# Decay rows by plain broadcasts, half-size differences and other small moves of order in a hybrid decoder layer

## The chip, the cores and the metric

The kernel runs on one core of a Trainium2 chip. The metric is the device time of one execution in microseconds (us); each kernel is run several times, and the median counts. Engines are named as in the profile: PE (TensorE, matmuls; PEld is its weight load), DVE (VectorE), ACT (ScalarE), POOL (GpSimd), SP (SyncE, whose in-order queue issues nearly all transfers).

## The reference

One decoder layer over 1024 tokens of width 1024, in float32. Two groups of heads read one input projection and mix tokens in parallel; their outputs are joined by one output projection, and a squared-ReLU MLP of hidden width 4096 follows.

```python
h = rms_norm(x, norm1_w)
proj = h @ w_in                      # q,k,v of 4 attention heads; q,k,v,z,a,b of 4 DeltaNet heads
# group A: differential attention, causal, two 64-d softmax maps per head, 128-d values
da_o = (softmax(q1 k1^T) - lam * softmax(q2 k2^T)) v     # then per-head rms_norm
# group B: gated DeltaNet: causal conv (width 4) + SiLU on q,k,v, L2-normed q,k, decay g, strength beta
#   chunked delta rule; within a chunk decay[i,j] = exp(G_i - G_j) for j <= i, else 0 (G: running sum of g)
x = x + concat(da_o, dn_o) @ w_out
x = x + square(relu(rms_norm(x, norm2_w) @ w_up)) @ w_down
```

## The kernel before, in words

Every large product is made in three matmuls of float32 parts: each operand is split into a rounded part (`hH`, `wH`, by a cast on ACT) and the rest (`hL`, `wL`, by a subtraction on DVE or POOL), and PE adds high x high, high x low and low x high. So each weight tile is loaded by SP (`wraw`, `raw`, `dw`), cast by ACT, subtracted, then used.

The stages in order of time, with where they lie in the profiled execution:

- *Norm and gate projection* (0 to 60 us). Blocks of 128 tokens: `z_norm(tb)` squares on ACT, takes the power on POOL and scales on DVE (L249) to `hn`; `to_hT` transposes it on PE; `z_part(tb, u)` multiplies by two weight units `wz[0]`, `wz[1]`, rounded by `z_round` (ACT, L317) and `z_rest` (DVE, L321); `z_gate` reads the bank out (L309 to L313). In this stage PE, DVE and ACT run in the order of the program. The pool `pj` has two PSUM banks.
- *DeltaNet projection* (60 to 232 us). `dn_units` projects one head and one half of the tokens per unit `n` (24 matmuls, L202 to L204), frees the bank by a copy to `cp` on ACT (L525), runs the convolution on ACT and DVE (L527, L529). `keys`, `queries` and `values_in` follow one unit behind (`skew`): transposes, a product of keys with keys or queries, the decay mask, and tiles parked in DRAM (`park`). `decay_rows(h)` prepares for a head a tile `dts[h]` of 128 x 1024: the mask `after` (0 or -1e30) plus the running sum `cgr_d`, read back from DRAM to all partitions. `decay` applies the exponential in place on ACT (L585). Heads 0 and 1 come first as keys (n = 0 to 3) and queries (4 to 7), then heads 2 and 3 (8 to 15), then values. From n = 12 on, steps of a triangular inversion on DVE (`invert`) are put between the units. The order of the engines here comes from the framework's own simulation of the program; each engine's queue then runs in order.
- *Inverse, scan, attention, output projection* (232 to 640 us). PE's order is written out by a planner, `Interleave`: streams (`horner` for the inverse, `scan`, `values`, `scores`, `da_turns`, `da_units`, `outproj` and others) yield the time from which their next piece may run, the planner keeps a model clock with costs such as `powr`, `act`, `vec`, and always takes the first stream that is ready. `da_units` projects q and k of the attention, with weights in two halves `w[0]`, `w[1]` (`first_w` is the first, loaded in the stage before); `da_turns` transposes q and k; `leave` holds the next block while more than two turns wait (`late`). Other engines follow the framework's order.
- *Second norm and seam* (600 to 660 us). `norm2` scales each half of a block; `turn_b` transposes; `read_first` reads the first square product out of banks `X0` and `Y`.
- *MLP up* (640 to 944 us) and *down* (944 to 1259 us), as seven products instead of eight (sums and differences of quarter matrices). In the down part `down` multiplies halves `s` of hidden units: `split4` splits the activations `ur` and the weight `wd[n][s]` in two pieces each, 48 matmuls follow into four banks (`bankA` or `bankB`), then DVE adds the banks to the accumulators `accs` (L1684), which were loaded back by `load_acc`. Differences of weights (b - a and so on) are made in place by `both` on whole tiles (L1705). SP's queue holds, in this order, activations, all eight accumulators, then weights d and c:

```python
    with tc.issue_after(last.ins):
        load_acc()
        for n in "dc":
            for s in range(2):
                dn_raw(0, n, s)
```

## Time and profile before

| | |
|---|---|
| median of 3 runs | 1261.04 us (1260.59 to 1262.15) |
| profiled execution | 1260.75 us; its span, from first to last instruction, 1259.0 us |
| mean granted TensorE clock | 0.996 |
| busy: PE, DVE, ACT, POOL | 1226.7, 834.3, 614.9, 147.1 us |
| moved by DMA | 201.27 MB, mean 160 GB/s |

A row of waits reads: the waiting engine, its tile and line, the engine, tile and line that released it, total us, times, longest. A row of a timeline reads: start, duration, engine, line, operation, output and input; in brackets the idle time before it and who ended it. A row of stretches gives the length, the busy us of each engine with instruction counts, the granted clock, the DMA share and GB/s. Matmul ends are modelled and overlap the next, so a single matmul shows about 0.39 us although one starts every 0.22 us.

### The profile page before, as it was taken

Reading aid. Unit: us, or ns where it says so; the run is one execution under the profiler, and the core shown is the slowest. Engines: PE = TensorE matmul, PEld = TensorE weight load, DVE = VectorE, ACT = ScalarE, POOL = GpSimd, SP = SyncE. Lnnn points to the kernel's source line nnn. Section 1 sums busy time; section 2 is a strip of 40 time slices with the busy share of each in tenths; the row PEclk is TensorE's granted clock in tenths of the full one; section 3 lists DMA queues with packets and bytes.
Section 4 is the critical chain, followed back from the end, with each engine's and each line's share of the span. In section 5 each row is a group of like instructions: output and inputs, shape, how many; then the busy total and the mean of one; then the engine's idle time right before and its main releaser. Section 6 shows DMA issues by size and latency. Waiting matters only on the chain.

```text
span 1259.0 us, 17761 instructions
## 1 busy us (share of the span) xinstructions
PE 1226.7 (97%) x6338; PEld 1027.0 (82%) x6338; DVE 834.3 (66%) x1425; ACT 614.9 (49%) x1216; POOL 147.1 (12%) x185
## 2 busy tenths in 40 slices
PE   8997999999899999999999999999999999999998
PEld 7985888887777887888878888888888788888887
DVE  5555879558877658765799555665566865687553
ACT  5347555424456545645667444454563333333331
POOL 1111210113442132202310000000000000000000
PEclk9999999999999999999999999999999999999999
DMA  7176551457665657333446534534368755422301
GB/s 254 50 181 177 148 146 54 116 158 232 192 196 150 204 181 234 94 85 97 167 135 208 199 142 154 184 138 147 118 235 320 297 200 200 167 101 100 132 36 67
DMA packets 164655, 201.27 MB, mean 160 GB/s; under 512 B 20608, under 2 KB 124376, under 8 KB 164568
## 3 DMA queue, kind: packets, MB, share of 16 engines
q1 hardware_dynamic: 163992, 198.05, 47.9%
q0 software_dynamic: 576, 2.10, 0.8%
q8 instruction: 50, 0.82, 0.3%
q14 instruction: 37, 0.30, 0.1%
HBM read 132.45 MB, written 65.55 MB: 157 GB/s over the span
## 4 chain that ended last, share of the span: by engine, by line
PE 83%; DMA 6%; DVE 5%; ACT 2%; issue 2%; SPq 1%; POOL 1%; DVEq 0%; POOLq 0%; ACTq 0%
PE X L1382 4%; PE X L1381 4%; PE X L1383 4%; PE X L1678 3%; PE X L1679 3%; PE X L1677 3%; PE ps_dn L202 3%; PE ps_dn L203 3%; PE ps_dn L204 3%; PE ps_qk L943 3%; PE ps_qk L945 3%; PE ps_qk L944 3%; PE Y L1382 2%; PE Y L1381 2%; PE Y L1383 2%; PE ps_o L1127 2%
## 5 line engine op out<-in xcount | busy, mean ns | idle before, releaser
L1300 ACT CAST hH<-ur 128x1024 fp32r<-128x1024 f32 x56 | 58.5, 1049 | 175.7 <-PE Z L1678 85.2
L1301 DVE TENSOR_TENSOR hL<-ur,hH 128x1024 fp32r<-128x1024 f32 x56 | 68.4, 1224 | 83.3 <-ACT hH L1300 83.2
L1301 DVE TENSOR_TENSOR op<-raw,op 128x1024 fp32r<-128x1024 f32 x48 | 58.7, 1224 | 74.8 <-PE X L1382 40.9
L1678 PE MATMUL X<-hL,hH 128*128 128x512 f32 x224 | 87.6, 391 | 2.8 <-DVE hL L1301 2.8
L1677 PE MATMUL X<-hH 128*128 128x512 f32 x224 | 87.5, 391 | 1.4 <-DVE b L1579 1.4
L1679 PE MATMUL X<-hH,hL 128*128 128x512 f32 x224 | 87.3, 390 | 0.0
L202 PE MATMUL ps_dn<-hH,wH 128*128 128x512 f32 x192 | 76.5, 399 | 6.9 <-ACT cp L525 5.8
L943 PE MATMUL ps_qk<-wH,hH 128*128 128x512 f32 x192 | 82.1, 428 | 0.2 <-ACT wH L196 0.2
L203 PE MATMUL ps_dn<-hL,wH 128*128 128x512 f32 x192 | 76.4, 398 | 0.0
L944 PE MATMUL ps_qk<-wL,hH 128*128 128x512 f32 x192 | 75.5, 393 | 0.5 <-DVE wL L197 0.4
L945 PE MATMUL ps_qk<-wH,hL 128*128 128x512 f32 x192 | 75.9, 395 | 0.0
L204 PE MATMUL ps_dn<-hH,wL 128*128 128x512 f32 x192 | 75.8, 396 | 0.0
L1301 DVE TENSOR_TENSOR hL<-dw,hH 128x1024 fp32r<-128x1024 f32 x56 | 68.1, 1220 | 2.6 <-ACT hH L1300 2.6
L1300 ACT CAST op<-raw 128x1024 fp32r<-128x1024 f32 x48 | 50.3, 1051 | 35.0 <-PE Y L1383 19.9
L1300 ACT CAST hH<-dw 128x1024 fp32r<-128x1024 f32 x56 | 58.4, 1047 | 14.8 <-PE Z L1679 8.0
L529 DVE SCALAR_TENSOR_TENSOR cy<-cp,pv,cy 128x512 f32<-128x512 f32 x72 | 53.8, 749 | 10.5 <-ACT cy L527 10.0
L1085 ACT ACTIVATE pexp<-ps_sc,mx 128x128 f32<-128x128 f32 (+7 forms) x64 | 47.3, 741 | 24.3 <-DVE mx L1081 24.1
L196 ACT CAST wH<-wraw 128x512 fp32r<-128x512 f32 x64 | 37.3, 622 | 35.8 <-DMA wraw<-in_w_in_dram 24.8
L1081 DVE TENSOR_REDUCE mx<-ps_sc 128x1 f32<-128x128 f32 (+7 forms) x64 | 47.0, 754 | 10.8 <-PE ps_sc L1079 10.4
L1212 PE MATMUL ps_op<-wH,hH 128*128 128x512 f32 x128 | 54.0, 422 | 0.0
L1678 PEld LDWEIGHTS X<-hL,hH 128*128 128x128 f32 x224 | 42.2, 188 | 12.0 <-DVE hL L1301 3.2
L1677 PEld LDWEIGHTS X<-hH 128*128 128x128 f32 x224 | 42.3, 189 | 10.5 <-DVE b L1579 1.8
(358 smaller groups left out, 3445.7 us busy)
## 6 DMA issues: line engine op xcount, KB each, us to landing
ur<-ud SPq DMA_DIRECT2D x28, 1024.0 KB, 4.9
raw<-in_w_up_dram SPq DMA_DIRECT2D x32, 512.0 KB, 3.7
dw<-in_w_down_dram SPq DMA_DIRECT2D x32, 512.0 KB, 7.1
qk_d<-qa SPq DMA_DIRECT2D x32, 256.0 KB, 3.0
ud<-ua SPq DMA_DIRECT2D x16, 512.0 KB, 4.0
ud<-s SPq DMA_DIRECT2D x16, 512.0 KB, 2.6
wraw<-in_w_in_dram SPq DMA_DIRECT2D x24, 256.0 KB, 5.1
wraw<-in_w_in_dram SPq DMA_DIRECT2D x48, 128.0 KB, 2.7
```

Source lines behind the costliest of these rows:

```text
L202: T.matmul(ps, lh(k), rh(k), start=(k == 0), stop=False)
L203: T.matmul(ps, lh(k), rl(k), start=False, stop=False)
L204: T.matmul(ps, ll(k), rh(k), start=False, stop=(k == n - 1))
L943: T.matmul(ps, hH[:, 4 * kh + k, sl], wh[:, k, :], start=(kh + k == 0), stop=False)
L944: T.matmul(ps, hH[:, 4 * kh + k, sl], wl[:, k, :], start=False, stop=False)
L945: T.matmul(ps, hL[:, 4 * kh + k, sl], wh[:, k, :], start=False, stop=(kh + k == 4))
L1300: S.copy(dst[0], src)
L1301: V.tensor_tensor(dst[1], src, dst[0].bitcast(F32), ALU.subtract)
L1381: T.matmul(ps, op[0][:, k, cs], h[0][:, k, :], start=start and k == 0, stop=False, skip_group_check=True)
L1677: T.matmul(bank[t], v[0][:, j, sl], v[2][:, j], start=s0, stop=False, skip_group_check=True)
L1678: T.matmul(bank[t], v[0][:, j, sl], v[3][:, j], start=False, stop=False, skip_group_check=True)
L1679: T.matmul(bank[t], v[1][:, j, sl], v[2][:, j], start=False, stop=s1, skip_group_check=True)
```

## The change

Parts, from the front of the program to its end:

1. `z_norm(2)` stands after the second of four `z_round`/`z_rest` pairs of unit 1, not after the fourth.
2. `decay_rows`: SP reads the running sum from `cgr_d` straight to all partitions, and POOL adds the mask by a `tensor_tensor` of 128 x 1024; before, SP wrote the mask into the tile and a transfer of POOL's queue added the sum. Only heads 0 and 1 are prepared ahead of the projection; heads 2 and 3 at units n = 4 and n = 6, behind the last parked tile in SP's queue.
3. The second half of the first attention weights (`first_w`) is loaded and split at the end of the projection; before, at the start of `da_units`.
4. In the planner, the inverse's products start from 8000 ns instead of 5000, and a turn of q or k is due 2000 ns after its input instead of 500.
5. `norm2` scales both halves by DVE; before, for the first four blocks the second half went through ACT and POOL. The planner's cost of the power there is 1800 ns.
6. `read_first` runs in three pieces between other work of the seam.
7. Down: `bankA` starts with `Z`; the first half product fills banks two at a time; four accumulators are loaded ahead of weight d and four behind it; differences are made per piece within `split4`.

```diff
@@ -378,7 +378,8 @@
         for i in range(4):
             z_round(1, i)
             z_rest(1, i)
-        z_norm(2)
+            if i == 1:
+                z_norm(2)
         z_gate(0, 1, banks0[1])
         for tb in range(1, NT):
             for u in range(2):
@@ -546,8 +547,10 @@
             prev = it
         yield prev
 
+    parked = []
+
     def park(h, hf, slot, src):
-        nc.sync.dma_start(park_d[h, 4 * hf:4 * hf + 4, :, slot, :].rearrange("c p d -> p c d"), v4(src))
+        parked.append(nc.sync.dma_start(park_d[h, 4 * hf:4 * hf + 4, :, slot, :].rearrange("c p d -> p c d"), v4(src)))
 
     def cols4(t, h, hf):
         return t[:, 8 * h + 4 * hf:8 * h + 4 * hf + 4]
@@ -575,8 +578,8 @@
 
     def decay_rows(h):
         dts[h] = sa.tile([P, SEQ], F32, tag="dtm", name="dtm", bufs=4)
-        nc.sync.dma_start(v4(dts[h]), after.unsqueeze(1).broadcast_to([P, NT, P]))
-        G.dma_start(dts[h], cgr_d[h * SEQ:(h + 1) * SEQ].partition_broadcast(P), accum_op=ALU.add)
+        nc.sync.dma_start(dts[h], cgr_d[h * SEQ:(h + 1) * SEQ].partition_broadcast(P))
+        G.tensor_tensor(v4(dts[h]), v4(dts[h]), after.unsqueeze(1).broadcast_to([P, NT, P]), ALU.add)
 
     def decay(h, hf):
         for c in range(4 * hf, 4 * hf + 4):
@@ -584,7 +587,7 @@
             cs = slice(c * P, (c + 1) * P)
             S.activation(dts[h][:, cs], dts[h][:, cs], AF.Exp, bias=ncg[:, i:i + 1])
 
-    for h in range(HEADS):
+    for h in range(2):
         decay_rows(h)
     fx = sf.tile([P, 1024], F32, name="fx")
     fg = sf.tile([P, 1024], F32, name="fg")
@@ -670,10 +673,14 @@
         (queries, keys, values_in)[kind](h, hf, o)
         for _ in range(0 if n < 12 else 2 if n < 16 else 4):
             next(inverse, None)
+        if n in (4, 6):
+            with tc.issue_after(parked[-1].ins):
+                decay_rows(n // 2)
         if n == 22:
-            first_w = load_unit(w_in_v, [(512, 256), (0, 256)], 0, 4, eng=V, rp=sf)
+            first_w = [load_unit(w_in_v, [(512, 256), (0, 256)], 0, 4, eng=V, rp=sf)]
     for _ in inverse:
         pass
+    first_w.append(load_unit(w_in_v, [(512, 256), (0, 256)], 4, 4, eng=V, rp=sf))
 
     s1ctx.close()
     p1ctx.close()
@@ -723,7 +730,7 @@
                     nc.sync.dma_start(v4(gbs[h][bs, :])[:, :, bs], fsg_d[p0:p0 + 4, :].rearrange("c (r k) -> r c k", k=32))
 
         loads(0)
-        at = [flow.now + 5000] * HEADS
+        at = [flow.now + 8000] * HEADS
         for hf in range(2):
             for h in range(HEADS):
                 r = yield from flow.bank("px", at=at[h])
@@ -893,7 +900,7 @@
             while not late:
                 yield flow.now + 50, None
             g, kind, tb, qn, t = late[0]
-            r = yield from flow.bank("px", at=max(t + 500, qa_free[i % 2] - 500))
+            r = yield from flow.bank("px", at=max(t + 2000, qa_free[i % 2] - 500))
             late.pop(0)
             pt = px.tile([P, 512], F32, tag="px", name="ps_qkt")
             T.transpose(pt[:, 0:P], qn[:, 0:P], ident)
@@ -921,7 +928,7 @@
         def half_w(src, ranges, k0):
             return load_unit(src, ranges, k0, 4, eng=V), unit_time("V", 610.0)
 
-        w = [(first_w, [0.0] * 4), half_w(w_in_v, todo[0], 4)]
+        w = [(w, [0.0] * 4) for w in first_w]
         freed = [0.0, 0.0]
         for i in range(3):
             if i == 1:
@@ -1234,17 +1241,9 @@
             rstd(r, ss[:, 0:1], 1.0 / DM, EPS, None, "nrt", 1)
             for i in range(2):
                 sl = slice(512 * i, 512 * i + 512)
-                if i == 0 or pos >= 4:
-                    normed_by[:] = [V.scalar_tensor_tensor(hn[i], accs[tb][:, sl], r, w2b[:, sl], ALU.mult, ALU.mult)]
-                else:
-                    S.activation(hn[i], accs[tb][:, sl], AF.Copy, scale=r)
-                    G.tensor_tensor(hn[i], hn[i], w2b[:, sl], ALU.mult)
-            t = flow.chain(act(512, True), act(512, True), vec(1), vec(1), powr(1))
-            if pos >= 4:
-                return hn, flow.chain(vec(512, 60), vec(512, 60), start=t - flow.HOP)
-            flow.chain(vec(512, 60), start=t - flow.HOP)
-            t = flow.chain(act(512), ("G", 1230.0), start=t - flow.HOP)
-            return hn, t
+                normed_by[:] = [V.scalar_tensor_tensor(hn[i], accs[tb][:, sl], r, w2b[:, sl], ALU.mult, ALU.mult)]
+            t = flow.chain(act(512, True), act(512, True), vec(1), vec(1), ("G", 1800.0))
+            return hn, flow.chain(vec(512, 60), vec(512, 60), start=t - flow.HOP)
 
         w0 = pre[0]
         w1 = load_unit(w_out_v, [(512, 512)], 4, 4), unit_time()
@@ -1418,10 +1417,13 @@
     def read_first():
         a0 = pools["uz"].tile([P, 2, 512], F32, tag="ua0", name="ua0")
         S.copy(a0, banks["X0"])
+        yield
         V.tensor_tensor(a0, a0, banks["Y"], ALU.add)
+        yield
         act2(a0)
         nc.sync.dma_start(ud[1][0], a0)
         u[0] = {"a": a0}
+        yield
 
     def act2(t, src=None):
         S.activation(t, t if src is None else src, AF.Relu)
@@ -1514,14 +1516,17 @@
 
     held(0, [0, 1])
     held(1, [0, 1])
+    first = read_first()
+    next(first)
     held(2, [0, 1])
     combine(0, 5)
     rounded(0, 5)
     held(0, [2, 3])
     held(1, [2])
+    next(first)
     rest(0, 5)
     held(1, [3])
-    read_first()
+    next(first)
     combine(0, 6)
     rounded(0, 6)
     combine(0, 3)
@@ -1617,7 +1622,7 @@
     octx.close()
 
     ur = ctx.enter_context(tc.tile_pool(name="ur", bufs=1, **right))
-    bankA = [X[0][:, 0], X[0][:, 1]] + Z
+    bankA = Z + [X[0][:, 0], X[0][:, 1]]
     bankB = [X[1][:, 0], X[1][:, 1], Y[:, 0], Y[:, 1]]
     views = [x[:, ks, ts] for ts, ks in ((tok1, k1), (tok1, k2), (tok2, k1), (tok2, k2)) for x in (hH, hL)]
     w_dn = w_down[0].rearrange("(s g h q p) c -> p s g h q c", p=P, q=2, h=2, g=2)
@@ -1650,15 +1655,18 @@
             return nc.sync.dma_start(urs[max(m - 1, 0) % 4].rearrange("p (g q) t -> p g q t", g=2),
                                      ud[i][g0:g0 + 2].rearrange("g p q t -> p g q t"))
 
-    def load_acc():
-        for tb in tiles:
+    def load_acc(tbs):
+        for tb in tbs:
             nc.sync.dma_start(accs[tb], acc_d[tb])
 
-    def split4(dst, src):
+    def split4(dst, src, made=None):
         for j in (0, 2):
-            split([x[:, j:j + 2] for x in dst], src[:, j:j + 2])
-
-    def down(kg, wd, i, flip, n, out, start, stop):
+            js = slice(j, j + 2)
+            if made:
+                V.tensor_tensor(src[:, js], made[0][:, js], made[1][:, js], ALU.subtract)
+            split([x[:, js] for x in dst], src[:, js])
+
+    def down(kg, wd, i, flip, n, out, start, stop, made=None):
         bank = bankB if flip ^ (kg % 2) else bankA
         final = kg == NK - 1 and i == 4
         for s in range(2):
@@ -1667,9 +1675,10 @@
             m = halves.index((kg, i, s))
             raw = urs[max(m - 1, 0) % 4]
             split4(v[0:2], raw)
-            split4(v[2:4], wd[n][s])
+            split4(v[2:4], wd[n][s], made and [wd[x][s] for x in made])
             u_raw(m + 4 if m else 1)
             seq = [(j, t) for t in range(4) for j in range(4)] if final and s else \
+                [(j, t) for ts in ((0, 1), (2, 3)) for j in range(4) for t in ts] if m == 0 else \
                 [(j, t) for j in range(4) for t in range(4)]
             for j, t in seq:
                 sl = slice(t * P, t * P + P)
@@ -1693,31 +1702,25 @@
     for m in (2, 3, 4):
         last = u_raw(m)
     with tc.issue_after(last.ins):
-        load_acc()
-        for n in "dc":
-            for s in range(2):
-                dn_raw(0, n, s)
+        load_acc(tiles[:4])
+        for s in range(2):
+            dn_raw(0, "d", s)
+        load_acc(tiles[4:])
+        for s in range(2):
+            dn_raw(0, "c", s)
     for kg in range(NK):
         wd = wds[kg]
 
-        def both(dst, l, r):
-            for s in range(2):
-                V.tensor_tensor(wd[dst][s], wd[l][s], wd[r][s], ALU.subtract)
-
         down(kg, wd, 1, 0, "a", (0, lo), True, False)
-        both("b", "b", "a")
-        down(kg, wd, 5, 1, "b", (1, hi), True, False)
-        both("b", "d", "b")
-        down(kg, wd, 6, 0, "b", (0, hi), False, False)
+        down(kg, wd, 5, 1, "b", (1, hi), True, False, "ba")
+        down(kg, wd, 6, 0, "b", (0, hi), False, False, "db")
         down(kg, wd, 3, 1, "d", (0, hi), False, True)
-        both("a", "b", "a")
-        down(kg, wd, 7, 0, "a", (1, hi), False, False)
+        down(kg, wd, 7, 0, "a", (1, hi), False, False, "ba")
         down(kg, wd, 2, 1, "c", (0, lo), True, True)
         if kg + 1 < NK:
             for s in range(2):
                 dn_raw(kg + 1, "a", s)
-        both("b", "c", "b")
-        down(kg, wd, 4, 0, "b", (1, lo), False, True)
+        down(kg, wd, 4, 0, "b", (1, lo), False, True, "cb")
         if kg + 1 < NK:
             for n in "bdc":
                 for s in range(2):
```

## The prediction

> **What bounds the kernel now.** I read the page's summary of busy time first, then the list of waits with TensorE (PE) as the waiting engine, then the table of stretches with the granted clock, and only for the stalls that came out of these the order of time on the other engines.
>
> ```profile
> span 1259.0 us, 17761 instructions
> PE 1226.7 (97%) x6338; PEld 1027.0 (82%) x6338; DVE 834.3 (66%) x1425; ACT 614.9 (49%) x1216; POOL 147.1 (12%) x185
> ```
>
> PE is busy 97% of the span, so the change, which takes no matmul away, can only win the idle remainder, 1259.0 - 1226.7 = 32.3 us, and what a lowered clock adds to the busy part. The waits of PE say where most of the 32.3 us lies (columns: total us, times, longest):
>
> ```profile
> PE ps_dn L202 <- ACT cp L525: 5.8, 2, 4.6
> PE ps_qkt L899 <- DVE qn L986: 3.0, 1, 3.0
> PE X L1678 <- DVE hL L1301: 2.8, 1, 2.8
> PE ps_qkt L899 <- DVE qa L906: 1.8, 1, 1.8
> PE ps_tr L235 <- DVE hn L249: 1.5, 1, 1.5
> PE X L1677 <- DVE b L1579: 1.4, 1, 1.4
> PE ps_dn L202 <- ACT wH L196: 1.0, 1, 1.0
> ```
>
> The table of stretches shows what follows a long stall (columns: length, PE, PEld, DVE, ACT, POOL busy, then PEclk, DMA share, GB/s):
>
> ```profile
> 80.00:116.00 36.00, 28.74 (x133) 22.57 (x132) 19.41 (x42) 20.67 (x66) 6.43 (x8) 0.95 0.92 237
> 102.00:106.00 4.00, 3.15 (x8) 2.53 (x9) 1.99 (x7) 4.00 (x18) 0.71 (x1) 0.57 1.10 356
> 240.00:260.00 20.00, 19.30 (x158) 15.14 (x157) 10.23 (x23) 6.11 (x16) 5.69 (x6) 1.00 0.66 182
> 285.00:345.00 60.00, 53.84 (x328) 46.82 (x327) 50.02 (x129) 29.12 (x80) 25.42 (x25) 0.97 0.68 217
> 298.00:302.00 4.00, 3.99 (x28) 3.70 (x29) 3.29 (x9) 0.02 (x1) 3.31 (x4) 1.00 1.03 350
> 331.00:335.00 4.00, 4.00 (x20) 3.72 (x20) 2.14 (x4) 2.50 (x5) 0.00 (x0) 0.57 0.31 87
> 345.00:640.00 295.00, 290.21 (x1645) 240.47 (x1645) 205.95 (x475) 176.43 (x462) 77.83 (x94) 1.00 0.52 160
> 600.00:640.00 40.00, 39.45 (x207) 32.51 (x206) 30.08 (x62) 30.47 (x71) 11.02 (x14) 1.00 0.56 189
> 992.00:998.00 6.00, 6.00 (x20) 4.75 (x21) 6.00 (x7) 0.70 (x1) 0.00 (x0) 0.72 0.90 326
> 1020.00:1040.00 20.00, 20.00 (x90) 16.57 (x89) 11.26 (x12) 8.01 (x8) 0.00 (x0) 1.00 0.54 196
> ```
>
> The stalls of 4.6, 3.0 and 2.8 us are each followed by a clock of 0.57, 0.57 and 0.72, that is 4 x 0.43 = 1.7, 1.7 and 6 x 0.28 = 1.7 us lost as slow "busy" time; after the 1.8 us stall (298) the clock is 1.00. So removing a stall of 2.8 us or more is worth its length plus 1.7 us. At full clock a matmul takes 20.00 / 90 = 0.22 us (last row).
>
> **The change part by part.**
>
> *Decay rows.* Now SP fills each of the four row tiles with the mask, in 512-byte pieces, and GpSimd's (POOL's) queue adds the cumulative row on top by an accumulating transfer.
>
> ```profile
> 77.50 0.33 SPq L480 DMA_DIRECT2D cgr_d<-cgr  x1
> 78.41 4.83 SPq L578 DMA_DIRECT2D dtm<-after  x4
> 83.28 9.20 SPq L194 DMA_DIRECT2D wraw<-in_w_in_dram  x6
> dtm<-after SPq DMA_DIRECT2D x4, 512.0 KB, 5.7
> dtm<-cgr_d POOLq DMA_DIRECT2D x4, 512.0 KB, 10.6
> w1b<-in_norm_w_dram SPq DMA_DIRECT2D x1, 512.0 KB, 6.8
> 95.66 0.62 ACT L196 CAST wH<-wraw 128x512 fp32r<-128x512 f32 x1 [8.59 <-DMA wraw<-in_w_in_dram]
> 101.18 0.62 ACT L196 CAST wH<-wraw 128x512 fp32r<-128x512 f32 x1 [4.90 <-DMA wraw<-in_w_in_dram]
> 102.24 0.56 ACT L525 COPY cp<-ps_dn 128x512 f32<-128x512 f32 x1
> ```
>
> Eight transfers of 512 KB keep the DMA engines full; the six weight loads behind them take 9.20 us only to issue; ACT sits 8.59 and 4.90 us in front of weights that have not come, and the copy cp that would free PE's bank is queued behind these casts. That is the 4.6 us stall, and its echoes: 36.00 - 28.74 = 7.3 us idle in this stretch plus 1.7 us of clock, 9.0 us in all. The change leaves two plain 512 KB broadcasts at this place, of the kind of the w1b row (6.8 us to landing). What it adds: the broadcast reads cgr_d, so SP's in-order queue now waits until the store issued at 77.50 has landed, and the weight loads wait behind it. A 16 KB store of this kind lands in 1.5 us:
>
> ```profile
> fsx_d<-lt SPq DMA_DIRECT2D x32, 16.0 KB, 1.5
> L831 POOL TENSOR_TENSOR zgt<-zgt,dnwb 128x512 f32<-128x512 f32 x8 | 10.7, 1336 | 20.0 <-DMA zgt<-zg_d 20.0
> L986 DVE TENSOR_TENSOR qn<-qn,rn x32: 408/426/1517, 251.8 to 474.9; 128x256 f32<-128x256 f32 x32
> ```
>
> So SP is free at about 79.5, two issues later (2 x 0.4) at 80.3 against 83.28 now: the wait costs less than the four mask issues it replaces. Then 1 MB of rows and 1.5 MB of weights at the 356 GB/s of the stretch 102:106 take 7.0 us: weights there by 88, and the cast that waited ended its wait at 95.66. On POOL four additions of 128x1024 appear, 2 x 1.34 = 2.7 us each; the first two run about 87 to 92, before the head's exponentials, which stand right behind cp at 102.24 now. If that cover were gone, ACT would wait at the exponentials with cp behind, as now. I take 8.5 of the 9.0 us; ends 4 and 9.
>
> Heads 2 and 3 are asked for four and six units into the projection, behind a parked tile on SP; a head is needed four units later. Each unit is 24 matmuls, 5.3 us, so 21 us stand against 6.8 + 2.7 us. On POOL small memsets and powers queue behind an addition that waits for its transfer; nothing on PE reads them within a unit. Nothing, ends -2 and 0.
>
> *Norm of the third block two rounds earlier.* PE waits 1.5 us for hn L249. On ACT its square now overtakes two of the four casts L317 (2.21 / 4 = 0.55 us each) and so comes 1.1 us sooner, but the two DVE subtractions that it overtakes lie behind it from then on, in front of the gate that frees the bank of PE's next product:
>
> ```profile
> 16.80 2.21 ACT L317 CAST wH<-wraw 128x520 fp32r<-128x520 f32 x4
> 22.58 0.16 DVE L313 COPY ab<-ps_z 128x8 f32<-128x8 f32 x1
> PEld ps_z L302 <- DVE zg L311: 0.5, 1, 0.5
> ```
>
> That bank came free at 22.74, and PE's next product already met it late (0.5 us, last row). It comes no sooner than now, so of the 1.1 us only a part is kept. Gain 0.3, ends 0 and 1.5.
>
> *Second half of the first attention weights loaded in the projection.* PE idles 0.7 us in 240:260, in front of these weights. Casts and subtractions move, none are added; on SP four loads (the six above took 9.20 us when the engines were full) may stand in front of the inverse's small ones, which the planner now takes 3 us later. Gain 0.6, ends -1 and 0.7.
>
> *The written-out order* (inverse's products 3 us later, turning of q and k 1.5 us later). Only the order of PE's work moves. In 285:345 PE idles 6.2 us, and 1.7 us go to the clock: 7.9. The two turns L899 (3.0 + 1.7 and 1.8) are what a later turn meets: DVE's qn was late, its slowest 1517 against a median 426 ns. A turn 1.5 us later shortens the 3.0 us stall below the 1.8 us that left the clock alone, and removes most of the other: up to 1.5 + 1.7 + 1.5 = 4.7. The new order will put something else early; I take off 1.2. Gain 3.5, ends -6 (as many new stalls of the size seen here) and 7.9.
>
> *Second norm wholly on DVE.*
>
> ```profile
> L1238 DVE SCALAR_TENSOR_TENSOR hn<-acc,nr,w2b x12: 746/750/752, 604.6 to 642.4; 128x512 f32<-128x512 f32 x12
> L1241 POOL TENSOR_TENSOR hn<-hn,w2b x4: 1289/1378/1709, 605.0 to 626.9; 128x512 f32<-128x512 f32 x4
> ```
>
> Four times 0.75 us more on DVE, which is busy 30 of 40 us there; four POOL products and their ACT scalings go. The second half no longer waits 1.38 us for POOL, while the planner now allows 1.8 us for the power in place of 0.47. PE loses 0.55 us in 600:640. Nothing, ends -3 and 2.5, which also stand for the rest of 345:640 (4.8 us idle) in its new order. The first square product's combination, spread out, feeds banks nobody waits for: nothing.
>
> *Down projection.* The first product starts in Z instead of X, whose last reader is b L1579: the 1.4 us goes, since X is now needed 24 matmuls (5.3 us) later. The 2.8 us stall comes from this order:
>
> ```profile
> 959.83 9.03 SPq L1655 DMA_DIRECT2D acc<-acc_d  x8
> 969.87 11.03 SPq L1642 DMA_DIRECT2D dw<-in_w_down_dram  x8
> 982.84 2.29 DVE L1705 TENSOR_TENSOR dw<-dw 128x2048 f32<-128x2048 f32 x1 [2.73 <-DMA dw<-in_w_down_dram]
> 986.19 4.49 DVE L1705 TENSOR_TENSOR dw<-dw 128x2048 f32<-128x2048 f32 x2
> ```
>
> Weight d lands behind eight accumulator loads, and DVE then makes whole differences (2.29 us, the next two in front of the operand that PE waits for). Now four loads (about 4.5 us of the 9.03) come off ahead of d, and differences are made in halves right ahead of their use. Both sides of the wait move by more than 2.8 us, so it goes with its clock: 1.4 + 2.8 + 1.7 = 5.9. The added difference sits in the chain of each half product (six DVE operations of half of 2.29 us, 6.9 of the 10.7 us that PE takes for 48 matmuls, and the evacuations beside them); without that slack every half would lose the excess. Gain 5.8, ends 3 and 5.9.
>
> Sum: 8.5 + 0.3 + 0.6 + 3.5 + 0 + 5.8 = 18.7 us. The profiled execution took 1260.75 us, 0.29 below the median of the three runs (1261.04): 1242.05, or 1242.3 against the median. I say 1242.
>
> **Two rules against rows.** By the rows, stalls of 2.8 and 3.0 us also lowered the clock. The Trainium skill, page "TensorE: Matmul & The Clock Gate", section "What's actually happening", says the clock halves only after an idle window of about 3.4 us. By that rule only the 4.6 us stall would give 1.7 us back, and the sum would be 15.3: 1245.7. The trace disagrees, with 0.57 and 0.72 after the two shorter stalls.
>
> The L986 row above has one execution of 1517 ns beside a median of 426; POOL's zgt product was running. The Trainium skill, page "SBUF — State Buffer", section "SBUF: two separate sides", has a GpSimd operation hold the port pair that a VectorE operation with two SBUF inputs needs, so that one waits for the whole other; by that rule the trace agrees.
>
> **The rivals.**
> - *The new order of PE loses what it should win.* For: DVE is busy 50 of 60 us in 285:345, little room. Against: the stretch idles 6.2 us in all now. With -2 to -6 instead of +3.5: 1247.5 to 1251.5. Chance 0.25.
> - *The stall moves rather than goes at the decay rows.* DVE held by POOL's additions, or ACT at exponentials whose rows are late. Four additions of 2.7 us put at most 10.7 us in DVE's way, against 36.0 - 19.4 = 16.6 us idle there. If half of it reached PE: 1247.4. Chance 0.12.
> - *Every stall of these stretches goes.* 9.0 + 1.5 + 0.6 + 7.9 + 2.5 + 5.9 = 27.4: 1233.6. With most of it 1234 to 1238. Chance 0.12.
> - *Slower.* The projection holds its next block while more than two turns wait; with 32 turns each 1.5 us later up to 48 us of PE time must be filled by the scan, the inverse and the scores. It decides once more than 18.7 + 2.5 = 21.2 us, 14 of 32 turns, find no filler; all of it gives 1290. Against: the stretch lost 7.9 us with every cause counted. Chance 0.03.
> - *It does nothing that can be measured*, the gains given back later: the stalls after 640 come from their own transfers, not from earlier lateness. 1261. Chance 0.02.
>
> **How the numbers follow.** My case, 1238 to 1246, has 0.46. Range 1234 to 1252: it takes in nearly all of the first three rivals and leaves out the last two and the tails of the sums. A measurement of this kernel can tell about 0.2% (2.5 us) from no change: faster 0.95, same 0.02, slower 0.03.
>
> **What would show it.** In the changed trace the cast L196 near 95 no longer waits for its load, PE has no wait for cp L525, and the stretch from 80 to 116 has under 1 us idle at clock 1.00. The waits at b L1579 and hL L1301 are gone from the first down products. The waits at L899 are under 1.8 us. The prediction is wrong if SP sits at the broadcast for many us with weight loads behind, if PE waits for the row tile's exponentials, or if new waits of over 2.8 us stand between 230 and 640.

## The result, and the profile after

The changed kernel takes 1245.34 us (median of 4 runs, 1243.77 to 1246.93) against 1260.82 us of the kernel before, run beside it: a ratio of 0.9876, 95% interval 0.9859 to 0.9894, or 15.5 us less. Its profiled execution has a span of 1245.2 us, 13.8 us shorter than the one before.

The page's summary of busy time, after:

```profile
PE 1221.7 (98%) x6338; PEld 1025.5 (82%) x6338; DVE 843.6 (68%) x1445; ACT 611.1 (49%) x1212; POOL 145.5 (12%) x181
```

PE's busy time fell by 5.0 us with the same 6338 matmuls: that is the clock, which before was low behind three long stalls. The rest is idle time. Some of the waits of PE, after:

```profile
PE ps_tr L235 <- DMA mt<-mixa_d: 2.7, 2, 1.5
PE ps_t L567 <- DVE k L539: 1.7, 1, 1.7
PE ps_z L302 <- DVE ab L313: 0.6, 1, 0.6
PE ps_tr L235 <- DVE hn L249: 0.6, 2, 0.4
```

Of the seven waits shown before, only the one for `hn` is left, and shorter. None that is there now is longer than 1.7 us. The stretches that answer to those before:

```profile
20.00:60.00 40.00, 38.85 (x325) 38.10 (x324) 23.96 (x53) 17.67 (x40) 5.18 (x14) 1.00 0.26 78
80.00:116.00 36.00, 34.30 (x176) 28.84 (x175) 33.30 (x65) 24.95 (x78) 10.10 (x9) 1.00 0.58 175
228.00:645.00 417.00, 403.32 (x2448) 338.72 (x2446) 291.57 (x687) 222.40 (x589) 107.93 (x125) 1.00 0.54 163
285.00:345.00 60.00, 56.19 (x343) 48.59 (x341) 50.12 (x132) 27.94 (x73) 25.85 (x26) 1.00 0.69 217
350.00:470.00 120.00, 115.15 (x625) 93.85 (x625) 80.12 (x202) 69.16 (x184) 36.67 (x45) 1.00 0.62 189
935.00:1000.00 65.00, 65.00 (x288) 53.85 (x287) 54.32 (x52) 26.69 (x27) 0.00 (x0) 1.00 0.87 326
```

And four of the same stretches before, which the prediction did not show:

```profile
20.00:60.00 40.00, 38.52 (x323) 37.97 (x322) 22.58 (x51) 16.41 (x37) 5.22 (x14) 1.00 0.27 77
228.00:645.00 417.00, 404.60 (x2447) 339.16 (x2446) 290.52 (x678) 226.15 (x595) 116.06 (x130) 1.00 0.54 165
350.00:470.00 120.00, 118.52 (x637) 97.02 (x635) 78.86 (x202) 67.88 (x186) 35.61 (x45) 1.00 0.59 179
935.00:1000.00 65.00, 60.87 (x261) 49.56 (x260) 47.50 (x41) 27.09 (x28) 0.00 (x0) 0.97 0.87 325
```

Subtracting the PE column from the length gives the idle time. It fell from 1.48 to 1.15 us in the gate projection, from 7.26 to 1.70 at the decay rows and from 4.13 to 0 in the down part; from 228 to 645 us it *rose*, from 12.40 to 13.68, although the stretch of the turns within it, 285 to 345, fell from 6.2 to 3.8. With 1.7 us of clock back at each of the three stalls (each of these stretches now stands at 1.00), the sum is 0.33 + 5.56 + 4.13 - 1.28 + 5.1 = 13.84 us, which is the difference of the spans. So the front and the down part won, and the middle, where the order was rewritten, gained nothing but its clock.

The order of time at the decay rows, after (start, duration, engine, line, operation):

```profile
78.77 0.33 SPq L481 DMA_DIRECT2D cgr_d<-cgr  x1
79.21 1.40 SPq L194 DMA_DIRECT2D wraw<-in_w_in_dram  x3
80.71 0.89 SPq L581 DMA_DIRECT2D dtm<-cgr_d  x2
87.54 7.14 DVE L530 SCALAR_TENSOR_TENSOR cy<-cp,pv,cy 128x512 f32<-128x512 f32 x4
87.94 5.41 POOL L582 TENSOR_TENSOR dtm<-dtm,after 128x1024 f32<-128x1024 f32 x2 [30.40 <-DMA dtm<-cgr_d]
95.34 0.66 PE L567 MATMUL ps_t<-ident,k 128*128 128x128 f32 x4 [1.70 <-DVE k L539]
```

SP's wait for the store of `cgr_d` cost nothing that shows: three weight loads fill it, and the two broadcasts are out at 81.6. What is left is the last row's 1.70 us. PE waits there for `k`, which DVE makes after four convolution steps `cy`; these took 7.14 us, from 87.5 to 94.7, and POOL's two additions ran from 87.9 to 93.3. Two of the four steps took 0.75 us as before; the two that started beside an addition took 2.8 and 2.9 us.

### The profile page after: what moved, and what is told of

Its sections match the earlier page's. It is cut to its first block, busy times and chain, and to the rows that moved or that the text cites. A ratio compares the mean times of both kernels' runs of the same rounds, so it can differ in the third digit from the quotient of the medians.

```text
span 1245.2 us, 17736 instructions
## 1 busy us (share of the span) xinstructions
PE 1221.7 (98%) x6338; PEld 1025.5 (82%) x6338; DVE 843.6 (68%) x1445; ACT 611.1 (49%) x1212; POOL 145.5 (12%) x181
## 4 chain that ended last, share of the span: by engine, by line
PE 83%; DMA 5%; DVE 5%; ACT 2%; issue 2%; POOL 2%; SPq 1%; DVEq 0%; POOLq 0%; ACTq 0%
PE X L1382 5%; PE X L1380 5%; PE X L1381 5%; PE X L1687 4%; PE X L1686 4%; PE X L1688 4%; PE ps_dn L204 3%; PE ps_dn L202 3%; PE ps_dn L203 3%; PE Y L1382 2%; PE Y L1380 2%; PE Y L1381 2%; PE Y L1687 2%; PE Z L1687 2%; PE Y L1686 2%; PE Z L1686 2%
## 5 line engine op out<-in xcount | busy, mean ns | idle before, releaser
L530 DVE SCALAR_TENSOR_TENSOR cy<-cp,pv,cy 128x512 f32<-128x512 f32 x72 | 61.7, 859 | 5.9 <-ACT cy L528 5.2
L1221 PE MATMUL ps_op<-wH,hL 128*128 128x512 f32 x128 | 50.3, 393 | 0.0
L1220 PE MATMUL ps_op<-wL,hH 128*128 128x512 f32 x128 | 50.0, 391 | 0.0
L1380 PE MATMUL Y<-hH,op 128*128 128x512 f32 x128 | 49.8, 389 | 0.0
```

What stands on the lines that cost most here:

```text
L1380: T.matmul(ps, op[0][:, k, cs], h[0][:, k, :], start=start and k == 0, stop=False, skip_group_check=True)
```

## The experiments

Three kernels make one part of the change each, added to the kernel before; nine take one thing away from the changed kernel or alter it. Ratios are against the kernel before on the same chip (medians there 1261.02 us for the first four, 1262.14 for the next four, 1261.51 for the last four).

**The decay rows alone.** The kernel before with part 2.

```diff
+        nc.sync.dma_start(dts[h], cgr_d[h * SEQ:(h + 1) * SEQ].partition_broadcast(P))
+        G.tensor_tensor(v4(dts[h]), v4(dts[h]), after..., ALU.add)
-    for h in range(HEADS):
+    for h in range(2):
...
+        if n in (4, 6):
+            with tc.issue_after(parked[-1].ins):
+                decay_rows(n // 2)
```

> The kernel before with the decay rows alone changed (plain broadcasts, mask added on GpSimd, heads 2 and 3 later). Theory A, each part pays in its own stage: the stretch 80 to 116 goes from 7.3 us idle to about 1.7 and its clock dip of 1.7 us goes, so 7.3 us less, ratio 0.994; the later stalls (L899 of 3.0 us, hL L1301 of 2.8 us) stay. Rival B, the later stalls are late echoes of this one: they shrink too, and the ratio is 0.990 or lower.

Measured: 1257.09 us, 0.9972 [0.9953, 0.9991], 3.5 us less. PE no longer waits for `cp` near 102, and the 1.7 us for `k` is there. But a new stall appears at the end of the projection. Its rows in the order of time, SP's queue first:

```profile
225.32 3.17 SPq L728 DMA_DIRECT2D gb<-fsg_d  x7
234.53 1.48 SPq L194 DMA_DIRECT2D wraw<-in_w_in_dram  x3
238.02 0.50 PE L948 MATMUL ps_qk<-wH,hH 128*128 128x512 f32 x1 [3.29 <-ACT wH L196]
```

The stretch around it:

```profile
230.00:250.00 20.00, 16.46 (x102) 13.52 (x102) 9.95 (x20) 3.54 (x8) 3.44 (x4) 0.91 0.50 123
```

The second half of the attention weights is queued on SP behind 16 of the inverse's small loads `gb` (the first seven are shown), and PE now gets there before it: 3.29 us, and 20 x 0.09 = 1.8 us of clock. Most of what the front wins is lost again here. The inverse's products, asked for from 5000 here, do not wait for `gb`, although PE ended the projection 7.9 us sooner than before (223.88) and the first `gb` went out only 5.1 us sooner.

**The down part alone.** The kernel before with part 7.

```diff
-    bankA = [X[0][:, 0], X[0][:, 1]] + Z
+    bankA = Z + [X[0][:, 0], X[0][:, 1]]
...
-        load_acc()
+        load_acc(tiles[:4])
...
```

> The kernel before with the down projection alone changed (bank order, accumulators in two halves, differences per piece). Theory A: waits at b L1579 (1.4 us) and hL L1301 (2.8 us) and the clock dip after it (1.7 us) go, 5.8 us less, ratio 0.9954, all else as before. Rival B: the change only works on the earlier timing of the whole; here a new wait near 990 remains and the ratio is 0.998 to 1.000.

Measured: 1255.51 us, 0.9961 [0.9943, 0.9978], 4.9 us less. The stretch of the first down products:

```profile
935.00:1000.00 65.00, 65.00 (x288) 53.83 (x287) 54.69 (x53) 29.05 (x30) 0.00 (x0) 1.00 0.87 325
```

No idle time is left, as in the changed kernel. The part stands by itself, and its predicted 5.8 lies inside the interval (2.8 to 7.2 us).

**The order alone.** The kernel before with part 4.

```diff
-        at = [flow.now + 5000] * HEADS
+        at = [flow.now + 8000] * HEADS
-            r = yield from flow.bank("px", at=max(t + 500, qa_free[i % 2] - 500))
+            r = yield from flow.bank("px", at=max(t + 2000, qa_free[i % 2] - 500))
```

> The kernel before with only the two numbers of the written-out order changed (inverse from 8000, turns due after 2000). The prediction's step: 3.5 us less, ratio 0.997, the waits at L899 under 1.8 us. Theory A, from the trace after: the clock dip of 1.7 us goes but other waits come in the same stretch, net 0 to 2 us less, ratio 0.998 to 1.000. Rival: worse than before, ratio above 1.001.

Measured: 1270.81 us, 1.0074 [1.0048, 1.0101], 9.3 us *more*. PE's longest wait at the scores:

```profile
380.07 0.47 PE L1076 MATMUL ps_sc<-KS,qa 128*128 128x512 f32 x1 [2.32 <-DMA qa<-qk_d]
```

And the stretch of the scores:

```profile
350.00:470.00 120.00, 113.22 (x593) 92.46 (x592) 72.18 (x191) 61.69 (x174) 34.94 (x45) 0.97 0.57 170
```

The long waits at the turns are gone from the list as foreseen: from 285 to 345 us PE idles 2.9 us at full clock, where it idled 6.2 us and lost 1.7 to the clock. But 6.8 us of idle time with 120 x 0.03 = 3.6 us of clock stand at the scores instead, where the kernel before idles 1.5 us at full clock, and smaller losses are spread over the rest. Alone the new numbers are a loss.

**The old order in the changed kernel.** Part 4 taken back.

```diff
-        at = [flow.now + 8000] * HEADS
+        at = [flow.now + 5000] * HEADS
-            ... max(t + 2000, ...)
+            ... max(t + 500, ...)
```

> The changed kernel with the two old numbers of the written-out order (5000 and 500). If the new numbers give what the prediction took, this is 3.5 us slower than the changed kernel, about 1249, with waits of 2 to 3 us at L899 (here L906) again. If they give nothing, it is 1244 to 1247. If the new numbers cost something, below 1244.

Measured: 1260.98 us, 1.0007 [0.9986, 1.0027]: the whole gain of 15.5 us is gone, though decay rows and down part are as in the changed kernel. A wait of PE:

```profile
PE ps_p L739 <- DMA gb<-fsg_d: 4.5, 4, 2.6
```

SP's queue: the store of `fg`, the first load that reads it, and four loads of parked tiles with three more `gb` behind them:

```profile
220.18 0.33 SPq L611 DMA_DIRECT2D fsg_d<-fg  x1
225.04 0.33 SPq L730 DMA_DIRECT2D gb<-fsg_d  x1
233.08 1.85 SPq L780 DMA_DIRECT2D pka<-park_d  x4
234.97 1.38 SPq L730 DMA_DIRECT2D gb<-fsg_d  x3
```

The stretch around it:

```profile
230.00:250.00 20.00, 15.66 (x104) 12.87 (x104) 7.75 (x16) 2.33 (x7) 2.86 (x3) 0.91 0.48 119
```

Asked for 5 us after the stage's start, the inverse's products now come before their operands `gb`: 4.5 us of waits and 1.8 us of clock. This is a coupling that the prediction missed, but it is only 6.3 of the 16 us. At the scores (350 to 470 us) this kernel idles 5.7 us with 3.6 us of clock, against 4.9 us at full clock in the changed kernel. The turns wait again too, 3.8 us in sum with 2.1 the longest. None of the three cases written down foresaw a loss of this size. The same rows of the kernel before and of the changed kernel show where it comes from (the last product of the projection on PE; the store of `fg`, last step of the inversion on DVE; the first load `gb`). Before:

```profile
231.82 0.39 PE L204 MATMUL ps_dn<-hH,wL 128*128 128x512 f32 x1
226.19 0.45 SPq L608 DMA_DIRECT2D fsg_d<-fg  x1
230.44 1.27 SPq L723 DMA_DIRECT2D gb<-fsg_d  x3
```

After:

```profile
224.79 0.39 PE L204 MATMUL ps_dn<-hH,wL 128*128 128x512 f32 x1
222.51 0.33 SPq L611 DMA_DIRECT2D fsg_d<-fg  x1
227.38 0.33 SPq L730 DMA_DIRECT2D gb<-fsg_d  x1
```

PE ends the projection 7.0 us sooner, but the inversion, steps on DVE put between the units, ends only 3.7 us sooner, and `gb` 3.1. Asking for the products 3 us later gives back about the 4 us that PE is now ahead. (In the kernel with the old order PE's last product of the projection starts at 222.45, 9.4 us sooner than before, and `gb` 5.4 us sooner: again 4 us apart.) That the inversion on DVE is what makes `gb` late is not shown: with the decay rows alone PE was 2.8 us further ahead than `gb` without a wait for it, and PE's longest wait here, 2.6 us, ends at 239.1, behind the three `gb` that SP issued at 235.0 after the parked tiles.

**Only the inverse's number taken back** (turns at 2000).

```diff
-        at = [flow.now + 8000] * HEADS
+        at = [flow.now + 5000] * HEADS
```

> The changed kernel with the inverse's products from 5000 again, turns still due after 2000. Theory C, DVE holds the inversion back while PE's projection now ends 7 us sooner, so that 5000 asks for products before their small loads have come: waits of ps_p for gb of 3 to 5 us and a clock dip of 1.7 us near 230 to 240, 5 to 7 us slower than the changed kernel, 1250 to 1252. Rival D, the old order lost its time in the turns: within 2 us of the changed kernel.

Measured: 1264.15 us, 1.0021 [1.0004, 1.0037]. A wait of PE:

```profile
PE ps_p L739 <- DMA gb<-fsg_d: 4.2, 4, 2.4
```

The same wait as with both numbers taken back: it is the inverse's number that counts. The place was foreseen, the size was not: 5 to 7 us were expected and about 18 measured, by the ratios. Of that, 4.1 us of idle time and 20 x 0.17 = 3.4 us of clock stand from 230 to 250 us; from 350 to 470 us PE idles 10.4 us and loses 120 x 0.04 = 4.8 us to the clock, against 4.9 us in all in the changed kernel.

**Only the turns' number taken back** (inverse at 8000).

```diff
-            ... max(t + 2000, ...)
+            ... max(t + 500, ...)
```

> The changed kernel with turns due after 500 again, inverse still from 8000. Theory C: no waits of ps_p for gb over 0.6 us; the turns cost what is left of the 12.4 us by which the span of the old order was longer, 4 to 7 us, with waits for qn at the turns of 1.5 us and more. Rival D: all of the 12 us, 1257 or more. The prediction's step, taken on this kernel: 3 to 5 us slower.

Measured: 1246.28 us, 0.9863 [0.9845, 0.9881], which is the changed kernel's ratio within the intervals. One turn waits again, and the clock falls behind it:

```profile
341.05 0.30 PE L906 MATMUL ps_qkt<-ident,qn 128*128 128x128 f32 x1 [2.33 <-DVE qn L993]
```

The stretches behind it and of the scores:

```profile
340.00:345.00 5.00, 3.95 (x12) 3.25 (x13) 3.65 (x10) 1.59 (x4) 1.78 (x2) 0.67 0.55 186
350.00:470.00 120.00, 117.52 (x643) 97.01 (x642) 80.23 (x206) 69.94 (x188) 37.11 (x46) 1.00 0.61 186
```

So the later turn does remove a stall with its clock, 2.33 + 5 x 0.33 = 4.0 us; the scores pay 117.52 - 115.15 = 2.4 us of it back, and the rest goes in smaller waits. In sum it is worth nothing that the intervals can tell; all the values written down ahead, 3 us and more, were too high.

**The mask added on DVE.** The changed kernel with one word altered.

```diff
-        G.tensor_tensor(v4(dts[h]), v4(dts[h]), after..., ALU.add)
+        V.tensor_tensor(v4(dts[h]), v4(dts[h]), after..., ALU.add)
```

> The changed kernel with the mask added on DVE instead of GpSimd, same shapes. Theory E, the 1.7 us wait of PE for k near 95 comes from DVE's convolution being held by the two GpSimd additions (four of its operations took 7.14 us instead of 3.0): here they take 0.75 us each, and the wait at ps_t goes to under 0.5 us; against that DVE has four additions of about 1.2 us more, and the inversion may end some us later. Time 1243 to 1246. Rival F, the wait comes from the load or from ACT's place behind the rows: it stays at 1 us or more.

Measured: 1242.65 us (1240.74 to 1243.51), 0.9838 [0.9823, 0.9852]. DVE's rows in the order of time:

```profile
86.23 1.23 DVE L582 TENSOR_TENSOR dtm<-dtm,after 128x1024 f32<-128x1024 f32 x1 [0.25 <-DMA dtm<-cgr_d]
87.37 1.41 DVE L530 SCALAR_TENSOR_TENSOR cy<-cp,pv,cy 128x512 f32<-128x512 f32 x2
```

The projection:

```profile
60.00:220.00 160.00, 160.00 (x838) 136.09 (x837) 129.98 (x317) 94.45 (x289) 20.14 (x26) 1.00 0.48 140
```

DVE makes an addition in 1.23 us where POOL took 5.41 / 2 = 2.7, two `cy` steps take 1.41 us again, and PE is never idle in the projection. POOL's additions were the cause of the 1.70 us. This version beats both kernels: its interval lies below that of the change (0.9859 to 0.9894), and it took 1242.65 us where the changed kernel with the turns' old number, run on the same chip, took 1246.28.

**The second half of the weights late.** The changed kernel without part 3.

```diff
-    first_w.append(load_unit(w_in_v, [(512, 256), (0, 256)], 4, 4, eng=V, rp=sf))
...
-        w = [(w, [0.0] * 4) for w in first_w]
+        w = [(first_w, [0.0] * 4), half_w(w_in_v, todo[0], 4)]
```

> The changed kernel with the second half of the first attention weights loaded at the start of the attention projection, as before the change. Theory G, this load then stands behind the inverse's small loads on SP, which DVE keeps late, so PE waits 2 to 4 us for it with a clock dip of 1.7 us, as in the run with the rows alone (3.29 us): 3 to 6 us slower, 1249 to 1251. The prediction's step: 0.6 us slower, no wait over 1 us here.

Measured: 1258.27 us, 0.9962 [0.9946, 0.9977]. A wait of PE in the list, and its longest at the scores:

```profile
PE ps_qk L949 <- ACT wH L196: 3.8, 2, 3.2
379.02 0.74 PE L1082 MATMUL ps_sc<-KS,qa 128*128 128x512 f32 x1 [2.20 <-DMA qa<-qk_d]
```

The 3.2 us behind the `gb` loads are back, as with the decay rows alone, and the clock from 230 to 250 us is 0.83. That was foreseen. What makes the loss, 11 us by the ratios, larger than the 3 to 6 us written down is the scores, where PE idles 6.2 us and loses 4.8 to the clock. The kernel with the order alone has the same loss: from the first product of the attention projection to 480 us PE works on the same tiles in the same order in both, and waits 2.20 us here at the score where it waits 2.32 there. One has the changed front and the other has not, so this loss goes with the written-out order, whatever the front.

So parts 3 and 4 go together: with decay rows and down part as changed, 8000 without the early half gives a ratio of 0.9962, the early half with the old numbers 1.0007, both 0.9876; neither would give about 0.993, if decay rows alone and down part alone just add up (that kernel was not run).

**All four heads ahead.** The changed kernel, plain broadcasts for four heads at once.

```diff
-    for h in range(2):
+    for h in range(HEADS):
```

> The changed kernel with all four heads' rows prepared ahead of the projection, still by plain broadcasts and GpSimd additions. Theory H, the old stall came from the kind of the transfers (512-byte pieces and accumulation, eight transfers): with four plain ones, 2 MB, the weights still come in time (no wait of ACT for wraw over 2 us), but GpSimd's four additions of 2.7 us hold DVE for 10.7 us instead of 5.4, so PE waits 3 to 6 us near 90 to 105: 1248 to 1253. Rival I, the number of transfers ahead of the weights was what mattered: ACT waits for wraw again by 4 us or more.

Measured: 1251.35 us, 0.9924 [0.9904, 0.9944], about 6 us more than the change. The order of time:

```profile
81.70 2.17 ACT L196 CAST wH<-wraw 128x512 fp32r<-128x512 f32 x4
86.83 9.11 DVE L530 SCALAR_TENSOR_TENSOR cy<-cp,pv,cy 128x512 f32<-128x512 f32 x4
92.63 5.54 POOL L582 TENSOR_TENSOR dtm<-dtm,after 128x1024 f32<-128x1024 f32 x2
98.77 1.11 PE L567 MATMUL ps_t<-ident,k 128*128 128x128 f32 x4 [5.83 <-DVE k L539]
```

Four 512 KB transfers no longer make the weights late: the casts at 81.70 wait for nothing. It is POOL's four additions, one behind the other from 87.4 to 98.2 (the row shows the last two), that stretch the four `cy` to 9.11 us and the `k` behind them, and PE waits 5.83 us for `k`. From 98 to 106 us the clock is then 0.61, another 8 x 0.39 = 3.1 us.

**Accumulating transfers, two heads at a time.** The changed kernel with the old way of filling a tile.

```diff
-        nc.sync.dma_start(dts[h], cgr_d[...].partition_broadcast(P))
-        G.tensor_tensor(v4(dts[h]), v4(dts[h]), after..., ALU.add)
+        nc.sync.dma_start(v4(dts[h]), after...)
+        G.dma_start(dts[h], cgr_d[...].partition_broadcast(P), accum_op=ALU.add)
```

> The changed kernel with the old kind of transfers (mask by SP, sum added by an accumulating transfer of GpSimd's queue), two heads ahead and two at units 4 and 6. If the number ahead of the weights is what mattered (rival I): no wait near 95 over 1 us, DVE free, 1243 to 1246. Theory H: half of the old traffic still stands before the weights, ACT waits for wraw by 3 to 8 us and PE by 2 to 4 us: 1248 to 1253.

Measured: 1247.3 us, 0.9894 [0.987, 0.9918], the changed kernel's ratio within the intervals. Two stretches:

```profile
80.00:116.00 36.00, 36.00 (x190) 30.63 (x189) 30.37 (x73) 24.50 (x81) 7.18 (x9) 1.00 0.78 203
133.00:137.00 4.00, 3.68 (x16) 3.34 (x17) 2.78 (x4) 1.57 (x4) 0.92 (x1) 0.57 0.67 142
```

The order of time between them:

```profile
129.84 2.44 ACT L588 ACTIVATE dtm<-dtm,ncg 128x128 f32<-128x128 f32 x8 [6.58 <-DMA dtm<-cgr_d]
133.32 0.80 PE L202 MATMUL ps_dn<-hH,wH 128*128 128x512 f32 x1 [3.21 <-ACT cp L526]
```

Two heads instead of four cure the stall near 102 by themselves, with no idle time at all from 80 to 116. The price comes later: the mask and then the sum make head 2's tile late, ACT waits 6.58 us at its exponentials with `cp` behind, and PE 3.21 us plus 4 x 0.43 = 1.7 of clock. The plain broadcast saves that and pays 1.70 us at `k`.

**Eight accumulators ahead of weight d.** Halves of differences stay.

```diff
-        load_acc(tiles[:4])
+        load_acc(tiles)
...
-        load_acc(tiles[4:])
```

> The changed kernel with all eight accumulators loaded ahead of weight d, differences still made per piece. Theory J, either half of the change is enough for the stall at hL L1301: d lands about 978 instead of 973 in this kernel's time and PE does not wait, 1244 to 1247. Rival K, the load order was the cause: a wait of 2 to 3 us at the third product returns with 1.7 us of clock, 1249 to 1251.

Measured: 1244.28 us, 0.9863 [0.9843, 0.9883]; the stretch of the first down products has no idle time.

**Whole-tile differences.** The accumulators stay split, four and four.

```diff
+        def both(dst, l, r):
+            for s in range(2):
+                V.tensor_tensor(wd[dst][s], wd[l][s], wd[r][s], ALU.subtract)
...
-        down(kg, wd, 5, 1, "b", (1, hi), True, False, "ba")
+        both("b", "b", "a")
+        down(kg, wd, 5, 1, "b", (1, hi), True, False)
...
```

> The changed kernel with the differences made on whole tiles ahead of each product as before, accumulators still in two halves. Theory J: no wait of PE over 0.5 us between 940 and 1000, 1244 to 1247. Rival L, the long differences in front of the square and sum operations at the seam and of PE's operand were the cause: a wait of 1.5 us or more near 980 returns, 1247 to 1250.

Measured: 1244.04 us, 0.9865 [0.9846, 0.9884]. One small wait is back:

```profile
955.32 0.50 PE L1688 MATMUL X<-hH,hL 128*128 128x512 f32 x1 [0.53 <-DVE hL L1300]
```

Either half of the down change removes the 2.8 us stall without the other. I had credited both together ("both sides of the wait move by more than 2.8 us"), and each was enough. Both of these kernels keep the new bank order and the filling of banks two at a time; a kernel with those alone was not run.

## Why the prediction came out

The time, 1245.34 us, lies 3.3 us above the predicted 1242 and inside its case of 1238 to 1246, but two terms of the sum were mis-sized, and a third came out to a tenth partly by luck.

- *Decay rows, predicted 8.5, measured 5.56 + 1.7 = 7.3 us.* The stall of 4.6 us went with its clock. The sign "under 1 us idle" from 80 to 116 did not come: what is missing are the 1.70 us at `k`. They are the rival "DVE held by POOL's additions" in a mild form, and I had the row for it, the 1517 ns of L986, with a page of the Trainium skill beside it; I spread 10.7 us of additions over 16.6 us of idle DVE time, as if DVE could choose when to be held. The four `cy` stand in front of an operand of PE, and being held there is what counts. The mask added on DVE shows the cause, and four additions in a row show its size. By the Trainium skill, page "SBUF — State Buffer", section "SBUF: two separate sides", a GpSimd operation that reads SBUF and starts first locks out a VectorE operation with two SBUF inputs for its whole length; the rows agree (four `cy` in 7.14 and 9.11 us beside additions of 2.7, against 0.75 each). I also credited the plain transfer with the cure of the first stall; two heads instead of four do that alone, and so do four plain transfers.
- *Norm of the third block, predicted 0.3, measured 0.33.* The wait for `hn` shrank from 1.5 to 0.6 us in sum, and a new one of 0.6 us for `ab` L313 took its place: the bank in front of the next product, as argued.
- *The written-out order and the second half of the weights, predicted 3.5 + 0.6, with the second norm at nothing; measured together +0.4 us.* This is the step that failed: the term was worked out in the stretch as it was before, 7.9 us of stalls that a later turn would thin out. The turns' number did remove its stalls, and in sum it is worth nothing that can be measured. The 8000 and the early half act elsewhere, at the start of the stage and at the scores. Together they keep the gain of the front; without the early half 11 us of it go, and with the old number 16 to 18 (by the ratios). Beyond what the changed kernel loses there, 6 to 7 us of this, clock and all, stand at the start of the stage (230 to 250 us), where PE arrives before its weights or `gb`, and 4 to 10 at the scores (350 to 470 us); without the early half PE's order is one that loses at the scores with the old front too. The first rival named this place; its cause, DVE's "little room" from 285 to 345, is not the one that the runs showed.
- *Down, predicted 5.8, measured 4.13 + 1.7 = 5.8.* Alone it gives 4.9 us by time. The waits went as argued; that the 1.7 us of clock were there to be won is luck of the profiled execution, for with the decay rows alone the same stall of 2.80 us left the clock at 1.00.
- *Clock.* Each of the three stalls did give 1.7 us back in the profiled executions. The prediction's rule, a stall of 2.8 us or more is worth 1.7 us on top, does not hold in general: see the 2.80 us just named, and 1.83 us with the order alone that did lower the clock. The Trainium skill, page "TensorE: Matmul & The Clock Gate", section "What's actually happening", puts the idle window at about 3.4 us; here idle times of 1.83, 2.33 and 3.21 us were already followed by 0.72 over 6 us, 0.67 over 5 and 0.57 over 4. By that page's rule two of the three places would have given no clock back, 3.4 us less.

By terms, 18.7 predicted becomes 13.8: -1.2 at the decay rows, -3.7 in the middle, nothing elsewhere. The medians give 15.5; the profiled execution, 1246.93 us, was the slowest of the four.

Open: why PE idles 5.7 to 10.4 us at the scores (350 to 470 us) in four of the kernels (order alone, old order, the inverse's number, late half), with a longest wait of 2.2 to 2.9 us for `qa` from DRAM in each, against 1.5 us before and 4.9 after. That it comes with the order that the planner writes is shown for two of them, which share that order; which of the planner's costs or due times is wrong there wasn't tried. The norm of the third block, the second norm and the pieces of `read_first` were not run by themselves either.

## What to carry to other kernels

Time saved ahead of a hand-written order can be lost again behind it: look up when the operands of the next stage come and which queue brings them, and move the due times together with the saving, or a part of it returns as a wait, with the clock on top. A due time also reorders everything behind it, so follow the trace to the end of the stage; a third to a half of what a wrong number cost here stood 120 us and more behind it. Try such numbers together with what they belong to; alone they measured as a loss of 9.3 us here. An addition given to an idle engine isn't free if it holds another engine's operations: look at what stands in the held engine's queue at that very time, not at its idle time over the stretch.

## What the runs showed of the hardware

- POOL's addition of 128 x 1024 float32 with both inputs in SBUF takes 2.4 to 2.8 us against DVE's 1.23, and each made the DVE operation with two SBUF inputs that ran beside it last 2.7 to 2.9 us instead of 0.75 (0.69 for `k`): two of four `cy` beside two additions, 7.14 us in all, three of four `cy` and one `k` beside four.
- PE's clock fell after idle times of 1.83 us (order alone, below) and 2.33 us (turns' number taken back), by about 1.7 us of lost time, as much as after 4.6 us; after 5.83 us 3.1 us were lost. Yet 2.80 us (rows alone, below) left it at 1.00 from 990 to 1010 us. So the length of a stall between these two figures does not say whether the clock falls.

```profile
424.53 0.63 PE L1115 MATMUL ps_at<-ident,pexp 128*128 128x128 f32 x4 [1.83 <-DVE qa L906]
991.72 0.50 PE L1683 MATMUL X<-hL,hH 128*128 128x512 f32 x1 [2.80 <-DVE hL L1306]
```

- Four 512 KB reads of a row to all partitions ahead of the weights left no cast waiting; four masks and four accumulating transfers at the same place had left ACT waiting 8.59 and 4.90 us.
